# One multiplication of the feed-forward stage moved from GpSimd to VectorE, in a two-block transformer on one core

## The chip, the cores and the metric

The kernel runs on one core of a Trainium2 chip. The metric is the device time in microseconds, the median of the runs. A profiled execution also gives a trace of every engine: TensorE (PE, with its weight loads as PEld), VectorE (DVE), ScalarE (ACT), GpSimd (POOL) and the queue that issues transfers (SP).

## The reference, cut to what matters

Two transformer stacks of two layers each are computed one after the other in float32. The change lies in the feed-forward part of the first stack, which each of its two layers runs once:

```
hn = rms_norm(h, norm_ffn_g[l])
g, u = jnp.split(hn @ w_gu[l], [D_FF], axis=-1)
h = h + (jax.nn.silu(g) * u) @ w_down[l]
```

D_MODEL is 1024, D_FF is 2816 and there are 528 positions (16 meta tokens and 512 tokens; the second layer needs only the 512).

## The kernel before

Activations are stored transposed: 128 features on the partitions, positions along the row. A float32 product is made of three TensorE passes over operands split in a high and a low part (`mm3`, lines 96 to 98): high by high, high by low, low by high. Each split is a cast on ScalarE (`hi`) and a subtraction on VectorE (`lo`); for weights in `weight` that is L90 and L92, and in `split` L176 and L177.

D_FF is cut into 22 pieces of 128 features. `index(i)` makes piece i: gate and up product of it, silu of the gate, the product of the two, and its split into `yh` and `yl` for the down-projection. Pieces 0 to 2 are made in the plain way in `early`. Pieces 3 to 21 use the seven-product form: the gate and up weights and the two halves of the features and positions make a 2x2 by 2x2 block product, which needs seven block products instead of eight, at the price of sums of blocks.

- `halves4` loads the gate tile (r1) and the up tile (r2) of the piece and lets GpSimd make four sums of their blocks (L129 to L132). The sums go into `ws` and `ws4`, with one buffer each, and into r2 itself. Then r1, the sum `ws`, r2 and the sum `ws4` are split.
- `seven` runs the seven products, 12 matmuls of 264 (second layer: 256) columns each, in the order p1, p2, p6, p5, p7, p3, p4. p1 uses the PSUM bank "tr", p2, p5 and p3 use "mm" (three banks), and p6, p7 and p4 use "sc" (two banks). ScalarE copies p1 out (`u`, L159); VectorE adds the others up in the tile `quarters` (L161 to L172). p6 is taken out by L163, which also reads `u`. p4 gets the bank that p6 had.
- `index` then takes silu of the gate half on ScalarE (`sl`, L701, one buffer), multiplies it by the up half in place (L702), and splits the result into `yh` (ScalarE, L176) and `yl` (VectorE, L177).

The loop over `nf` in 5, 5, 4, 4, 4 makes one piece more than the down-projection needs next, and then runs the eight output tiles of the down-projection over `nf` pieces. So the seven-product forms come in runs of 3, 5, 4, 4 and 3 in each layer, with down-projections between them. Each engine works through its queue in order. The order in which the instructions of different pieces stand in a queue is fixed by a planner when the program is built; it need not be that of the source.

Of the kernel before, what the change touches and what calls it, by code (L numbers as in the profile page):

```python
# [46 lines left out]
def both_blocks(ctx: ExitStack, tc: tile.TileContext, xT, cst, par1, w1in, w1out, w1gu, w1dn, wgate,  # L47
                memT, pos, par2, rel, w2in, w2mix, w2mq, w2mkv, w2mo, w2f1, w2f2, out):
    nc = tc.nc
# [70 lines left out]
    def halves4(pool, w1, w2):  # L120


        r1 = wpool.tile([128, 8, 128], F32, name="wraw", bufs=3)
        nc.sync.dma_start(r1, w1)
        r2 = pool.tile([128, 8, 128], F32, name="wraw2", bufs=2)
        nc.sync.dma_start(r2, w2)
        s = pool.tile([128, 8, 128], F32, name="ws", bufs=1)
        s4 = pool.tile([128, 4, 128], F32, name="ws4", bufs=1)
        nc.gpsimd.tensor_add(s[:, 4:], r2[:, :4], r2[:, 4:])  # L129
        nc.gpsimd.tensor_sub(s[:, :4], s[:, 4:], r1[:, :4])  # L130
        nc.gpsimd.tensor_sub(r2[:, :4], r1[:, :4], r2[:, :4])
        nc.gpsimd.tensor_sub(s4, r1[:, 4:], s[:, :4])  # L132
        got = []
        for x in (r1, s, r2, s4):
            if x is s4:
                hi = pool.tile([128, 4, 128], F32R, name="wh4", bufs=1)
                lo = pool.tile([128, 4, 128], F32R, name="wl4", bufs=1)
            else:
                hi = wpool.tile([128, 8, 128], F32R, name="whi", bufs=3)
                lo = wpool.tile([128, 8, 128], F32R, name="wlo", bufs=3)  # L140
            split(hi, lo, x)
            got += [(hi[:, o:o + 4], lo[:, o:o + 4]) for o in range(0, hi.shape[1], 4)]
        return got

    def seven(pool, w, x, n, bufs):


        a11, a12, s2, s1, s3, a22, s4 = w
        b11, b21, t2, t1, t3, b22, t4 = x

        def product(ps, w, x):
            for k in range(4):
                mm3(ps, w[0][:, k], w[1][:, k], x[0][k], x[1][k], k == 0, k == 3)

        e = pool.tile([128, 4, n], F32, name="quarters", bufs=bufs)
        u = pool.tile([128, n], F32, name="u1", bufs=2)
        p1, p2, p6, p5, p7, p3, p4 = (bank(t)[:, :n] for t in ("tr", "mm", "sc", "mm", "sc", "mm", "sc"))
        product(p1, a11, b11)
        nc.scalar.copy(u, p1)  # L159
        product(p2, a12, b21)  # L160
        nc.vector.tensor_add(e[:, 0], p2, u)  # L161
        product(p6, s2, t2)
        nc.vector.tensor_add(e[:, 3], p6, u)  # L163
        product(p5, s1, t1)
        nc.vector.tensor_add(e[:, 1], p5, e[:, 3])
        product(p7, s3, t3)
        nc.vector.tensor_add(e[:, 2], p7, e[:, 3])
        nc.vector.tensor_add(e[:, 3], p5, e[:, 2])
        product(p3, s4, b22)
        nc.vector.tensor_add(e[:, 1], p3, e[:, 1])  # L170
        product(p4, a22, t4)
        nc.vector.tensor_add(e[:, 2], p4, e[:, 2])  # L172
        return e

    def split(hi, lo, x):
        nc.scalar.copy(hi, x)  # L176
        nc.vector.tensor_sub(lo, x, f(hi))  # L177
# [121 lines left out]
    for l in range(2):  # L299
# [3 lines left out]
        l0 = late[0][0]  # L303
        with ExitStack() as lay:
# [325 lines left out]
            with ExitStack() as ffn:  # L630
# [58 lines left out]
                def index(i):  # L689
                    if i < 3:  # L690
                        su = firsts[i][:, 2:4].rearrange("p a b -> p (a b)")
                    else:
                        with ExitStack() as order:
                            if i == 3:
                                for ins in after:
                                    order.enter_context(tc.issue_after(ins.ins))
                            w = halves4(ff, w1gu[l, 2 * i], w1gu[l, 2 * i + 1])
                        e = seven(ff, w, rhs, half, 3)
                        sg, su = (e[:, o:o + 2].rearrange("p a b -> p (a b)") for o in (0, 2))
                        sl = ff.tile([128, T], F32, name="sl", bufs=1)  # L700
                        nc.scalar.activation(sl[:, l0:], sg, AF.Silu)  # L701
                        nc.gpsimd.tensor_mul(su, su, sl[:, l0:])  # L702
                    hi = fy.tile([128, T], F32R, name=f"yh{i % 6}")
                    lo = fy.tile([128, T], F32R, name=f"yl{i % 6}")
                    split(hi[:, l0:], lo[:, l0:], su)
                    made.append((hi, lo))

                f0 = 0
                for nf in (5, 5, 4, 4, 4):
                    if l == 1 and f0 == 5:  # L710
                        tables()
                    while len(made) < min(f0 + nf + 1, 22):
                        index(len(made))
                    ys = made[f0:f0 + nf]
                    for m in range(8):
                        w = weight(w1dn[l, m, :, f0:f0 + nf], nf)
                        for p, a, b in proj(w, ys, late):
                            done = nc.vector.tensor_add(h[m][:, a:b], h[m][:, a:b], p)  # L718
                            if f0 + nf == 22 and m == 0:
                                ended = done  # L720
                    f0 += nf
# [619 lines left out]
```

## Time and profile before

| | |
|---|---|
| median of 3 runs | 2901.34 us (2901.32 to 2905.62) |
| the profiled execution, its own time | 2905.03 us |
| its span in the trace | 2903.2 us |
| PE busy | 2767.8 us (95%) |
| DVE busy | 1924.7 us (66%) |
| ACT busy | 1316.8 us (45%) |
| POOL busy | 679.7 us (23%) |

The median is what is forecast. The rows come from the profiled execution, so durations are compared with its own time. Busy shares are averages over stages with different limits. A busy PE is not PE at its peak, because matmuls overlap and their ends are modelled.

### The profile page before, as it was taken

The page shows a single profiled execution, that of the slowest core. Times are in us where ns is not written, and L with a number is a line of the kernel's source. Part 1 is how long each engine was busy: PE and PEld are TensorE (multiplying, and loading weights), DVE is VectorE, ACT ScalarE, POOL GpSimd, SP SyncE. Part 2 cuts the span into 40 slices and gives each one's busy share as a digit, 9 for nine tenths or more (in the row PEclk, how much of TensorE's full clock was granted, in tenths as well). Part 3 has the DMA queues.
Part 4 walks back from the last instruction along what each step waited for, and adds up shares of the span by engine and source line. Part 5 has one row for each costly group of instructions (what it writes and reads, how often), then busy time and mean ns, then how long its engine had stood idle before and what let it go on. Part 6 is the DMA issues. An engine that isn't in the chain of part 4 may idle for free.

```text
span 2903.2 us, 45359 instructions
## 1 busy us (share of the span) xinstructions
PE 2767.8 (95%) x17148; PEld 2445.7 (84%) x17148; DVE 1924.7 (66%) x3856; ACT 1316.8 (45%) x2362; POOL 679.7 (23%) x627
## 2 busy tenths in 40 slices
PE   8988999999998999999999999999999999999998
PEld 7988899999876888887789888888877898888887
DVE  7887756678888666667987564333689875643335
ACT  6664433336664433334675443332346754433323
POOL 0111544430012343432212031111322110311112
PEclk9999999999999999999999999999999999999999
DMA  4332223223332233335524223333245242233332
GB/s 149 83 82 88 67 89 94 88 80 103 97 88 84 82 93 89 90 92 141 157 64 129 87 66 95 97 98 96 80 131 148 64 133 81 66 102 94 95 94 66
DMA packets 101114, 277.35 MB, mean 96 GB/s; under 512 B 13856, under 2 KB 20512, under 8 KB 100896
## 3 DMA queue, kind: packets, MB, share of 16 engines
q1 hardware_dynamic: 100896, 274.45, 32.2%
q8 instruction: 136, 2.23, 0.3%
q14 instruction: 82, 0.67, 0.1%
HBM read 241.82 MB, written 2.10 MB: 84 GB/s over the span
## 4 chain that ended last, share of the span: by engine, by line
PE 57%; DVE 5%; issue 2%; ACT 2%; POOL 1%; ACTq 0%; POOLq 0%; DVEq 0%
PE mm L97 16%; PE mm L98 16%; PE mm L96 16%; PE sc L96 1%; PE sc L98 1%; PE sc L97 1%; DVE wlo L177 1%; PE av L96 1%; PE av L97 1%; PE av L98 1%; PE av L830 1%; PE bc L945 1%; PE tr L945 1%; DVE wlo L92 0%; ACT whi L176 0%
## 5 line engine op out<-in xcount | busy, mean ns | idle before, releaser
L96 PE MATMUL mm<-xh_all,whi 128*128 128x512 f32 (+2 forms) x2040 | 690.0, 341 | 18.9 <-ACT xh_all L316 8.1
L97 PE MATMUL mm<-xl_all,whi 128*128 128x512 f32 (+2 forms) x2040 | 694.3, 341 | 4.0 <-DVE xl_all L668 2.9
L98 PE MATMUL mm<-xh_all,wlo 128*128 128x512 f32 (+2 forms) x2040 | 688.4, 339 | 0.9 <-DVE wlo L92 0.8
L90 ACT CAST whi<-wraw 128x1024 fp32r<-128x1024 f32 (+2 forms) x416 | 391.3, 942 | 634.1 <-PE mm L97 587.7
L92 DVE TENSOR_TENSOR wlo<-wraw,whi 128x1024 fp32r<-128x1024 f32 (+2 forms) x393 | 460.4, 1172 | 212.9 <-ACT whi L90 210.4
L96 PEld LDWEIGHTS mm<-xh_all,whi 128*128 128x128 f32 x2040 | 390.5, 193 | 58.7 <-ACT xh_all L316 8.4
L97 PEld LDWEIGHTS mm<-xl_all,whi 128*128 128x128 f32 x2040 | 391.3, 192 | 43.6 <-DVE xl_all L668 5.1
L98 PEld LDWEIGHTS mm<-xh_all,wlo 128*128 128x128 f32 x2040 | 391.9, 192 | 36.0 <-DVE wlo L92 1.2
L1224 POOL TENSOR_TENSOR r<-r 128x512 f32<-128x512 f32 (+1 forms) x70 | 101.9, 1455 | 532.5 <-ACT r L1223 532.5
L96 PE MATMUL mm<-yh,whi 128*128 128x264 f32 (+1 forms) x528 | 169.7, 322 | 3.2 <-ACT yh L176 1.9
L97 PE MATMUL mm<-yl,whi 128*128 128x264 f32 (+1 forms) x528 | 169.9, 322 | 0.0
L98 PE MATMUL mm<-yh,wlo 128*128 128x264 f32 (+1 forms) x528 | 169.4, 321 | 0.0
L791 DVE TENSOR_TENSOR hall<-hall,mm 128x512 f32<-128x512 f32 (+1 forms) x82 | 46.6, 569 | 145.8 <-PE mm L98 145.5
L177 DVE TENSOR_TENSOR wlo<-wraw,whi 128x1024 fp32r<-128x1024 f32 x76 | 117.1, 1541 | 25.6 <-ACT whi L176 25.3
L96 PE MATMUL sc<-th,whi 128*128 128x264 f32 (+1 forms) x304 | 89.6, 295 | 31.7 <-DVE quarters L163 31.7
L96 PEld LDWEIGHTS mm<-yh,whi 128*128 128x128 f32 x528 | 99.0, 188 | 12.3 <-ACT yh L176 2.5
L97 PEld LDWEIGHTS mm<-yl,whi 128*128 128x128 f32 x528 | 99.2, 188 | 8.2 <-DVE yl L177 0.4
L98 PEld LDWEIGHTS mm<-yh,wlo 128*128 128x128 f32 x528 | 99.3, 188 | 8.0
L718 DVE TENSOR_TENSOR hall<-hall,mm 128x264 f32<-128x264 f32 (+1 forms) x120 | 61.1, 513 | 66.2 <-PE mm L98 65.9
L129 POOL TENSOR_TENSOR ws<-wraw 128x512 f32<-128x512 f32 x38 | 49.0, 1290 | 186.2 <-DVE wlo L177 117.0
L176 ACT CAST whi<-wraw 128x1024 fp32r<-128x1024 f32 x76 | 79.4, 1045 | 27.7 <-PE mm L97 26.0
L96 PEld LDWEIGHTS sc<-th,whi 128*128 128x128 f32 x304 | 58.7, 193 | 35.6 <-DVE quarters L163 35.4
(733 smaller groups left out, 7284.3 us busy)
## 6 DMA issues: line engine op xcount, KB each, us to landing
wraw<-w2f SPq DMA_DIRECT2D x128, 512.0 KB, 3.8
wraw<-w1gu SPq DMA_DIRECT2D x88, 512.0 KB, 3.6
wraw<-w2in SPq DMA_DIRECT2D x44, 512.0 KB, 4.0
wraw<-w1in SPq DMA_DIRECT2D x40, 512.0 KB, 3.6
wraw<-w2mkv SPq DMA_DIRECT2D x32, 512.0 KB, 3.6
wraw<-w1dn SPq DMA_DIRECT2D x48, 256.0 KB, 2.7
wraw<-w1dn SPq DMA_DIRECT2D x32, 320.0 KB, 3.0
wraw<-w1out SPq DMA_DIRECT2D x32, 256.0 KB, 2.7
```

The source lines that it names most:

```text
L90: nc.scalar.copy(hi[:, :kt], raw[:, :kt])
L92: (eng or nc.vector).tensor_sub(lo[:, :kt], raw[:, :kt], f(hi[:, :kt]))
L96: nc.tensor.matmul(ps, wh, xh, start=first, stop=False)
L97: nc.tensor.matmul(ps, wh, xl, start=False, stop=False)
L98: nc.tensor.matmul(ps, wl, xh, start=False, stop=last)
L129: nc.gpsimd.tensor_add(s[:, 4:], r2[:, :4], r2[:, 4:])
L176: nc.scalar.copy(hi, x)
L177: nc.vector.tensor_sub(lo, x, f(hi))
L718: done = nc.vector.tensor_add(h[m][:, a:b], h[m][:, a:b], p)
L791: nc.vector.tensor_add(X(m, a, b), X(m, a, b), p)
L945: nc.tensor.transpose(ps[:, 128 * j:128 * j + 128], p[:, 128 * j:128 * j + 128], ident)
L1224: nc.gpsimd.tensor_mul(r[:, a:b], r[:, a:b], r[:, a:b])
```

## The change

The multiplication of the silu of the gate by the up product (L702) is issued on VectorE instead of GpSimd, for the 19 pieces of each layer in the seven-product form. Operands, shapes and the place in the source stay.

```
                         sl = ff.tile([128, T], F32, name="sl", bufs=1)
                         nc.scalar.activation(sl[:, l0:], sg, AF.Silu)
-                        nc.gpsimd.tensor_mul(su, su, sl[:, l0:])
+                        nc.vector.tensor_mul(su, su, sl[:, l0:])
                     hi = fy.tile([128, T], F32R, name=f"yh{i % 6}")
                     lo = fy.tile([128, T], F32R, name=f"yl{i % 6}")
                     split(hi[:, l0:], lo[:, l0:], su)
```

## Rows read from the trace of the kernel before

**Rows 1.** The page: span, and busy time by engine.
```profile
span 2903.2 us, 45359 instructions
...
PE 2767.8 (95%) x17148; PEld 2445.7 (84%) x17148; DVE 1924.7 (66%) x3856; ACT 1316.8 (45%) x2362; POOL 679.7 (23%) x627
```
**Rows 2.** Windows: the runs of forms (a run, sums by layer), then products without waits.
```profile
core 0: us, PE busy (x) PEld busy (x) DVE busy (x) ACT busy (x) POOL busy (x), PEclk, DMA share, GB/s
...
391.64:449.26 57.62, 53.33 (x423) 52.69 (x421) 39.25 (x58) 23.52 (x33) 30.56 (x21) 0.97 0.28 81
...
sum 213.66, PE 199.93 PEld 197.79 DVE 150.81 ACT 88.56 POOL 106.25; mean PE 39.98 PEld 39.56 DVE 30.16 ACT 17.71 POOL 21.25
...
sum 216.48, PE 198.41 PEld 196.22 DVE 152.31 ACT 89.22 POOL 106.54; mean PE 39.68 PEld 39.24 DVE 30.46 ACT 17.84 POOL 21.31
...
401.89:409.19 7.30, 7.30 (x62) 7.30 (x61) 3.42 (x5) 2.38 (x4) 5.93 (x4) 1.00 0.26 74
1208.06:1213.78 5.72, 5.72 (x51) 5.72 (x49) 2.34 (x3) 1.45 (x2) 5.64 (x5) 1.00 0.30 82
```
**Rows 3.** Instructions of L163 (min/median/max ns), and who waited for them.
```profile
L163 DVE TENSOR_TENSOR quarters<-sc,u x38: 410/419/428, 337.0 to 1281.2; 128x264 f32<-128x264 f32 x19, 128x256 f32<-128x256 f32 x19
...
  PEld sc L96: 35.4, 18
  PE sc L96: 31.7, 18
```
**Rows 4.** TensorE at one stall: timeline, then windows after it (PEclk is third-last).
```profile
424.42 0.59 PE L96 MATMUL sc<-th,whi 128*128 128x264 f32 x1 [2.54 <-DVE quarters L163]
...
424.42:427.23 2.81, 2.81 (x13) 2.81 (x14) 2.73 (x6) 0.00 (x0) 1.06 (x1) 0.50 0.44 122
427.44:430.20 2.76, 2.76 (x24) 2.76 (x24) 2.20 (x3) 1.42 (x2) 2.68 (x3) 1.00 0.00 0
```
**Rows 5.** Timeline of GpSimd: start, duration, instruction, idle before it and releaser.
```profile
413.12 1.29 POOL L129 TENSOR_TENSOR ws<-wraw 128x512 f32<-128x512 f32 x1 [5.30 <-DVE wlo L177]
414.49 1.62 POOL L130 TENSOR_TENSOR ws<-ws,wraw 128x512 f32<-128x512 f32 x1
416.08 2.28 POOL L131 TENSOR_TENSOR wraw<-wraw,wraw 128x512 f32<-128x512 f32 x1
...
419.55 1.32 POOL L702 TENSOR_TENSOR quarters<-quarters,sl 128x528 f32<-128x528 f32 x1
426.17 1.28 POOL L129 TENSOR_TENSOR ws<-wraw 128x512 f32<-128x512 f32 x1 [5.29 <-DVE wlo L177]
```
**Rows 6.** Timeline of ScalarE in the same loop.
```profile
414.23 0.65 ACT L701 ACTIVATE sl<-quarters 128x528 f32<-128x528 f32 x1 [2.83 <-DVE quarters L170]
...
420.91 0.63 ACT L176 CAST yh<-quarters 128x528 fp32r<-128x528 f32 x1 [5.09 <-POOL quarters L702]
421.44 0.37 ACT L159 COPY u<-tr 128x264 f32<-128x264 f32 x1
```
**Rows 7.** Timeline of VectorE over two loops of the run from 391.64.
```profile
397.64 0.42 DVE L163 TENSOR_TENSOR quarters<-sc,u 128x264 f32<-128x264 f32 x1
...
398.70 1.22 DVE L177 TENSOR_TENSOR wlo<-ws,whi 128x1024 fp32r<-128x1024 f32 x1
...
402.09 0.43 DVE L172 TENSOR_TENSOR quarters<-sc,quarters 128x264 f32<-128x264 f32 x1 [0.18 <-PE sc L98]
403.09 2.30 DVE L177 TENSOR_TENSOR wlo<-wraw,whi 128x1024 fp32r<-128x1024 f32 x1 [0.57 <-ACT whi L176]
408.53 0.71 DVE L177 TENSOR_TENSOR yl<-quarters,yh 128x528 fp32r<-128x528 f32 x1 [3.13 <-ACT yh L176]
...
414.88 0.42 DVE L172 TENSOR_TENSOR quarters<-sc,quarters 128x264 f32<-128x264 f32 x1
...
423.94 0.43 DVE L163 TENSOR_TENSOR quarters<-sc,u 128x264 f32<-128x264 f32 x1
```
**Rows 8.** Groups by line: first matmuls of the down-projection, with their idle time.
```profile
L96 PE MATMUL mm<-yh,whi 128*128 128x264 f32 (+1 forms) x528 | 169.7, 322 | 3.2 <-ACT yh L176 1.9 <-DVE hall L718 1.3
```

More of the change, by code (lines that the diff above doesn't have):

```diff
@@ L701, in index @@
                         nc.scalar.activation(sl[:, l0:], sg, AF.Silu)
-                        nc.gpsimd.tensor_mul(su, su, sl[:, l0:])
+                        nc.vector.tensor_mul(su, su, sl[:, l0:])
                     hi = fy.tile([128, T], F32R, name=f"yh{i % 6}")
```

## The prediction

> **What bounds the kernel now.** I read the page first: TensorE is busy for 95% of the span, VectorE for 66% [rows 1]. The share says little about the stage of the change, so I turned to the two gate-and-up stages and timed the runs of seven-product forms on TensorE. A layer has 19 forms in five runs (3, 5, 4, 4 and 3 forms; between runs TensorE does the down-projection). The ten runs take 213.66 + 216.48 = 430.1 us [rows 2]. Where nothing is waited for, five products of layer 0 take 7.30 us, 1.46 each, and four of layer 1 take 5.72 us, 1.43 each [rows 2]. At that pace a form takes 7 x 1.46 = 10.2 us, and 38 forms take 133 x 1.46 + 133 x 1.43 = 384.4 us. So the runs hold 430.1 - 384.4 = 45.8 us that is not product work. This is the sum that the change can win, and it is 1.6% of the span.
>
> Who takes it: TensorE waits 18 times, 31.7 us in all (35.4 us by its weight loads), for L163 on VectorE [rows 3]. L163 empties the "sc" bank of the third product, and the seventh product needs that bank. In the large case TensorE idles 2.54 us, and then its granted clock is 0.50 (the 1.2 GHz level) for the next 2.81 us before it is 1.00 again [rows 4]; the twelve products' matmuls that need 1.46 us took those 2.81, so such a stall costs 1.35 us more. Of the 45.8 us, 35.4 are the waits; the other 10.4 are mostly such slow stretches (one is shown), and I allow 2 us of them for losses that have nothing to do with this loop.
>
> Why L163 is late: follow one loop backwards. L163 at 423.94 [rows 7] needs the copy u of the first product (L159). On ScalarE u stands in the queue right behind the cast yh, and yh waits 5.09 us for L702 [rows 6]. L702 starts at 419.55, directly behind the four sums of weights that stand ahead of it on GpSimd since 413.12 (6.43 us) [rows 5]. Its inputs were long there: sl (L701) was done at 414.88 [rows 6] and L172 at 415.30 [rows 7]. L702 itself takes 1.32 us. The next sums start at 426.17, because `ws` has one buffer, and wait for the VectorE split of the sums before [rows 5]. So the loop is sums, L702, yh, u, L161 to L163, split of ws, sums: 426.17 - 413.12 = 13.05 us, against the 10.2 us of TensorE. The loop sets the pace, and 18 loops with all four sums make the 18 stalls.
>
> **The change, part by part.** *GpSimd* loses 38 x 1.32 = 50 us of L702. GpSimd is not a bound by share; what counts is that its sums no longer stand ahead of the product.
>
> *VectorE* gains 38 multiplications of 128x528 (128x512 in layer 1), SBUF by SBUF. The nearest row is yl, the same shape and operands: 0.71 us, some 0.65 before the next one starts [rows 7]. That is 38 x 0.65 = 25 us on an engine that is idle for a third of the span. In a loop VectorE has now from 408.53 to 415.30 (6.8 us, 0.4 of it idle or held), plus one split wlo of 1.2: 7.6 us. With the product it has 8.2 us, under 10.2, so by its own work it stays hidden. If it were not, 0.65 would be added per loop.
>
> *The place on VectorE.* The queue's order before shows L172, the split wlo of the next form's third weight (403.09), yl [rows 7]. The product can only stand after L172 and before yl. Either place costs the same below. Its input sl is done when L172 ends, so it waits for nothing new, and yh follows it 4 to 5 us earlier than now, u directly behind.
>
> *Where the stall goes: the two engines' hold on each other.* A VectorE instruction with two SBUF operands and a GpSimd instruction do not run together here. L131 takes 2.28 us instead of L129's 1.29 when a wlo is in its way [rows 5], and wlo takes 2.30 instead of 1.22 when a sum is in its way [rows 7]. No longer hold is in these rows: each is held by one instruction of the other engine, then goes. L163, which reads PSUM, is never held: 410 to 428 ns over 38 [rows 3]. So the moved product meets the sums. The Trainium skill ("SBUF — State Buffer", section "SBUF: two separate sides") calls this an exclusive lock on a shared port pair, in which the loser blocks for the whole instruction, and this is a rule against the change; the trace agrees with it (2.30 against 1.22 us), and a rival below works out its worst case.
>
> I walk the run from 391.64 with turns taken one by one. The split of ws ends at 399.92 [rows 7] and L129 runs 400.06 to 401.36. L172 is 402.09 to 402.52. L130 ends at 403.03; the product is held until then and runs to 403.65. L131 runs to 404.90, wlo to 406.05, L132 to 407.30, yl to 407.90 (yh was done long before). Then come L161, wlo of the next first weight, and L163, ending at about 409.95. From the end of the split of ws to its next end is 11.5 us: 8.2 of own work and some 3.3 of holds. The seventh product wants L163 at 391.64 + 8.76 + 10.2 = 410.6, so the first loop has 0.65 us to spare (the 2.3 us lead that L163 of the first form had, ending 398.06 against 400.4 [rows 2, 7], absorbs the lag). The second loop then is 11.5 - 10.2 = 1.3 late, less 0.65: 0.6 us; a third is 1.3 late. A run of 3 has one full loop, of 4 two, of 5 three. So a layer keeps 0 + 1.9 + 0.6 + 0.6 + 0 = 3.1 us, two layers 6.2; with the 2 us that are not of this loop, 8 us stay. None of these stalls is as long as the 2.54 us that the slow clock followed, so the clock's part goes whole.
>
> *Ends of runs.* The down-projection waits 1.9 us in all for a yh [rows 8]; the product on VectorE ends about 0.65 us sooner and is not held by or behind sums. I take 1 us.
>
> *Bounds.* No row shows how the two engines share when the queues are this full. From below: if GpSimd always gives way, no loop is over 10.2 and the whole 45.8 plus 1.9 is won, 48 us. From above: no loop has lead, 18 x 1.3 = 23 us stay, and 22 us are won. The walk lies nearest to the first, as it uses this run's own rows: 45.8 - 8 + 1 = 39 us.
>
> **Does it reach the end?** TensorE is busy through 95% of the span [rows 1], and nothing outside the two stages is edited, so I let what TensorE gains there stay gained. The order of each queue is written when the program is built, from a plan that the trace does not show; I allow a few us either way for orders that change elsewhere.
>
> **The sum.** The profiled execution took 2905.0 us (span 2903.2 [rows 1] and 1.8 around it). 2905.0 - 39 = 2866. That execution is 3.7 us above the median of 2901.34, so on the median the forecast is **2862 us**.
>
> **Rivals.**
> (a) *The loop opens only in part.* yh may be queued on ScalarE behind a cast that waits for a sum (the casts of ws and wh stand near it). Then u still waits for some of the sums, about half of the 6.43 us, and half the gain is left: 2901 - 20 = 2881. For it: the order on ScalarE is not known. Against: yh becomes ready 4 us before those casts.
> (b) *No change: the holds take the place of the wait.* If all four sums hold VectorE for their whole length, the loop is 8.2 + 4 x 1.29 = 13.4 us, about today's 13.05, and the time is 2901 within 6. By the page's lock rule taken at its worst, this is the outcome. Against: L129 runs beside L167 to L170, which read PSUM and are not held, and part of L130 beside L172.
> (c) *Slower: VectorE paces every form, not only 18.* Today 20 forms lose almost nothing. If held-up VectorE work made all 38 run at one loop, the break-even is 10.2 + 45.8 / 38 = 11.4 us a form. At 11.5 it is 38 x 1.3 = 49 us of loss instead of 45.8, 3 us slower; at 13.4 it is 122 us, 2977 in all. For it: the walk's 11.5 is just over the point. Against: TensorE waits in only 18 of the 38 forms today [rows 3]; for the others the sums were made during the down-projection, or the next run's are not wanted yet, so nothing holds VectorE.
>
> **How the numbers follow.** Gain of 30 to 48 us: 0.70. Part of it, 6 to 30 us (a): 0.16. Within 0.2% (6 us, about what a measurement of this kernel can tell from no change) (b): 0.08. Slower (c), or by a worse order elsewhere: 0.06. So faster 0.86, same 0.08, slower 0.06. The range runs from the full 48 us (2853, less a us for scatter) to just past (a), at 2882; it leaves out some 2 in 10, nearly all above.
>
> **What would show it.** Right: L702 on VectorE at about 0.7 us, up to 2 when held; the ten runs together some 392 us instead of 430; waits of TensorE for L163 under 10 us and none above 2 us; granted clock 1.00 all through the runs; L129's starts in a run 10.2 to 11.5 us apart. Wrong: starts still 13 us apart (b), or yh on ScalarE still waiting 4 to 5 us (a), or waits in the first and last forms of the runs (c), or the runs shorter as said and the span not.

## The result, and the profile after

The changed kernel takes 2863.38 us (median of 4 runs, 2862.56 to 2867.84) against 2901.72 us before (4 runs, 2901.32 to 2905.62). The ratio is 0.9868, with a 95% interval of 0.9851 to 0.9885: 38.3 us less, where 39 were forecast. The profiled execution took 2867.84 us.

The first lines of the page of the changed kernel. VectorE gained 47 us of busy time [rows 1], more than the 25 us of its new instructions; the rest is holding, as below.

```profile
span 2866.1 us, 45365 instructions
...
PE 2761.2 (96%) x17148; PEld 2441.0 (85%) x17148; DVE 1971.8 (69%) x3894; ACT 1322.1 (46%) x2362; POOL 638.5 (22%) x589
```

Windows of its runs of seven-product forms: the run of five in layer 0, the first run of layer 1, and the sum for each layer (the third number from the right is the granted clock).

```profile
390.05:441.91 51.86, 51.43 (x423) 51.21 (x421) 47.20 (x62) 24.13 (x33) 26.82 (x17) 1.00 0.31 93
...
sum 196.12, PE 195.20 PEld 194.56 DVE 174.63 ACT 90.65 POOL 92.41; mean PE 39.04 PEld 38.91 DVE 34.93 ACT 18.13 POOL 18.48
...
952.45:984.07 31.62, 30.92 (x255) 30.20 (x253) 29.37 (x44) 16.60 (x25) 10.26 (x7) 1.00 0.32 93
...
sum 193.75, PE 191.88 PEld 190.19 DVE 177.91 ACT 91.47 POOL 92.87; mean PE 38.38 PEld 38.04 DVE 35.58 ACT 18.29 POOL 18.57
```

The ten runs take 196.12 + 193.75 = 389.9 us, where they took 430.1 [rows 2]. That is 40.3 us less, and 389.9 - 384.4 = 5.5 us that are not product work are left of 45.8. The granted clock is 1.00 in all ten. TensorE's waits for L163, by the view of that line, fell from 31.7 to 2.5 us [rows 3]:

```profile
  PEld sc L96: 4.1, 7
...
  PE sc L96: 2.5, 5
```

The same loop in the timelines of GpSimd, ScalarE and VectorE (start, duration, instruction, idle before and releaser):

```profile
409.60 1.29 POOL L129 TENSOR_TENSOR ws<-wraw 128x512 f32<-128x512 f32 x1 [4.19 <-DVE wlo L177]
410.97 1.64 POOL L130 TENSOR_TENSOR ws<-ws,wraw 128x512 f32<-128x512 f32 x1
412.57 1.76 POOL L131 TENSOR_TENSOR wraw<-wraw,wraw 128x512 f32<-128x512 f32 x1
414.28 2.27 POOL L132 TENSOR_TENSOR ws<-wraw,ws 128x512 f32<-128x512 f32 x1
420.74 1.29 POOL L129 TENSOR_TENSOR ws<-wraw 128x512 f32<-128x512 f32 x1 [4.19 <-DVE wlo L177]
...
413.21 0.64 ACT L176 CAST yh<-quarters 128x528 fp32r<-128x528 f32 x1 [0.91 <-DVE quarters L702]
413.75 0.37 ACT L159 COPY u<-tr 128x264 f32<-128x264 f32 x1
...
411.37 0.42 DVE L172 TENSOR_TENSOR quarters<-sc,quarters 128x264 f32<-128x264 f32 x1
411.89 1.28 DVE L702 TENSOR_TENSOR quarters<-quarters,sl 128x528 f32<-128x528 f32 x1
413.10 2.31 DVE L177 TENSOR_TENSOR wlo<-wraw,whi 128x1024 fp32r<-128x1024 f32 x1
415.33 1.79 DVE L177 TENSOR_TENSOR yl<-quarters,yh 128x528 fp32r<-128x528 f32 x1
...
418.51 0.42 DVE L163 TENSOR_TENSOR quarters<-sc,u 128x264 f32<-128x264 f32 x1
```

The product follows L172 at once, yh waits 0.91 us instead of 5.09 [rows 6], and L129's starts are 11.14 us apart instead of 13.05 [rows 5]. Now three VectorE instructions in a row meet the sums and are each held by one of them: 1.28 instead of 0.71 us, 2.31 instead of 1.22, 1.79 instead of 0.71.

### The profile page after: what moved, and what is told of

Read it like the earlier page. It is cut to its first block, busy times and chain, and to the rows that moved or that the text cites. A ratio compares the mean times of both kernels' runs of the same rounds, so it can differ in the third digit from the quotient of the medians.

```text
span 2866.1 us, 45365 instructions
## 1 busy us (share of the span) xinstructions
PE 2761.2 (96%) x17148; PEld 2441.0 (85%) x17148; DVE 1971.8 (69%) x3894; ACT 1322.1 (46%) x2362; POOL 638.5 (22%) x589
## 4 chain that ended last, share of the span: by engine, by line
PE 59%; DVE 5%; issue 1%; ACT 1%; POOL 0%; ACTq 0%; POOLq 0%; DVEq 0%
PE mm L97 17%; PE mm L98 16%; PE mm L96 16%; PE sc L96 1%; PE sc L98 1%; PE sc L97 1%; PE av L96 1%; PE av L97 1%; PE av L98 1%; PE av L830 1%; PE tr L945 1%; PE bc L945 1%; DVE wlo L92 0%; PE sc L951 0%; PE sc L952 0%
## 5 line engine op out<-in xcount | busy, mean ns | idle before, releaser
L92 DVE TENSOR_TENSOR wlo<-wraw,whi 128x1024 fp32r<-128x1024 f32 (+2 forms) x393 | 452.1, 1151 | 209.8 <-ACT whi L90 207.0
L130 POOL TENSOR_TENSOR ws<-ws,wraw 128x512 f32<-128x512 f32 x38 | 57.7, 1519 | 202.3 <-DMA wraw<-w1gu 200.1
L129 POOL TENSOR_TENSOR ws<-wraw 128x512 f32<-128x512 f32 x38 | 49.1, 1291 | 168.4 <-DVE wlo L177 98.4
```

The source lines that it names most:

```text
L92: (eng or nc.vector).tensor_sub(lo[:, :kt], raw[:, :kt], f(hi[:, :kt]))
```

## The experiments

Times are medians, beside the kernel before on the same chip (2903.1 us for the first four, 2901.7 for the next four, 2902.4 for the last three).

**The product first on GpSimd.** It stays there at full length, but the sums of the form after next are queued behind it:

```
-                made = []
+                made, muls = [], {}
...
-                            if i == 3:
-                                for ins in after:
+                            if i == 3 or i - 2 in muls:
+                                for ins in after if i == 3 else [muls[i - 2]]:
                                     order.enter_context(tc.issue_after(ins.ins))
...
+                        muls[i] = nc.gpsimd.tensor_mul(su, su, sl[:, l0:])
```

> The product stays on GpSimd, at its full 1.3 us, but stands ahead of the next sums in GpSimd's queue instead of behind them. Nothing else changes its place. Theory (the place in the queue behind four sums is the cost): the casts yh stop waiting 5 us, L129 starts 10.2 to 11.5 us apart instead of 13.05, TensorE's waits for L163 fall from 31.7 us to under 10, and the time is 2858 to 2875 us, about what the move to VectorE gave (2863). Rival 1 (what counts is that the product takes 0.7 us on VectorE instead of 1.3): little is won, 2890 us or more. Rival 2 (what counts is that GpSimd no longer holds VectorE with the product): little is won too, 2890 us or more, since GpSimd still runs it.

Measured: 2869.53 us, ratio 0.9888 (0.9871 to 0.9904). The order of the four other queues is that of the kernel before. GpSimd in this kernel, then the sums over the windows of the runs, layer 0 and layer 1:

```profile
399.14 1.32 POOL L702 TENSOR_TENSOR quarters<-quarters,sl 128x528 f32<-128x528 f32 x1 [6.03 <-DVE quarters L172]
400.43 2.27 POOL L129 TENSOR_TENSOR ws<-wraw 128x512 f32<-128x512 f32 x1
...
410.75 1.32 POOL L702 TENSOR_TENSOR quarters<-quarters,sl 128x528 f32<-128x528 f32 x1 [1.87 <-DVE quarters L172]
...
sum 197.63, PE 196.38 PEld 194.91 DVE 171.49 ACT 86.59 POOL 127.93; mean PE 39.28 PEld 38.98 DVE 34.30 ACT 17.32 POOL 25.59
...
sum 195.45, PE 192.53 PEld 190.36 DVE 172.65 ACT 87.55 POOL 128.03; mean PE 38.51 PEld 38.07 DVE 34.53 ACT 17.51 POOL 25.61
```

The product now stands ahead and waits for its own input, L172. The loop is 410.75 - 399.14 = 11.6 us and the runs take 197.63 + 195.45 = 393.1 us. So the place in the queue, without a change of engine or duration, wins 37 of the runs' 40 us. Both rivals are out.

**Half the product.** On GpSimd, behind the sums, with half of its columns left out:

```
+                        nc.gpsimd.tensor_mul(su[:, :half], su[:, :half], sl[:, l0:l0 + half])
```

> The product stays on GpSimd behind the sums, but multiplies only the first half of the columns; the other half is left out. Its time falls from 1.3 to some 0.7 us, as on VectorE. Theory (place in the queue): the loop gets 0.6 us shorter, 13.05 to 12.4, so of the 18 stalls 0.6 us each goes, 11 us, with a few us more where a shorter stall no longer brings the slow clock: 2880 to 2893 us. Rival 1 (the shorter duration is the gain): 2860 to 2870 us.

Measured: 2893.4 us, ratio 0.9965 (0.9953 to 0.9976), 0.4 us above the range of the theory. L702 takes 0.76 us here, and it is as late as before:

```profile
409.64 1.29 POOL L129 TENSOR_TENSOR ws<-wraw 128x512 f32<-128x512 f32 x1 [5.30 <-DVE wlo L177]
...
416.06 0.76 POOL L702 TENSOR_TENSOR quarters<-quarters,sl 128x264 f32<-128x264 f32 x1
422.11 1.29 POOL L129 TENSOR_TENSOR ws<-wraw 128x512 f32<-128x512 f32 x1 [5.29 <-DVE wlo L177]
```

The loop is 12.47 us. The shorter duration alone is worth about a quarter of the gain. The few us that the theory added for the clock did not come: five of the ten runs here still have a granted clock below 1.00, against six in the kernel before.

**The split behind u and L163.** The product stays on GpSimd, as late as before; its split is traced after L163 of the next form and queued behind u and L163:

```
         nc.vector.tensor_add(e[:, 3], p6, u)
+        if then:
+            with tc.issue_after(copied.ins), tc.issue_after(added.ins):
+                then()
```

> The product stays on GpSimd behind the sums, but the split of its result (yh on ScalarE, yl on VectorE) stands behind the copy u and behind L163 of the next form in those queues. The product is as late as before. Theory (the late product costs only because u, L161 and L163 are queued behind its split): L163 no longer waits for the product, the loop loses u, L161, the split of the first weight and L163, some 2.6 us, and comes to about 10.4 us, and the time is 2858 to 2875 us. Rival (the late product costs by something else, such as the buffers or the down-projection that wants yh): no gain, 2895 us or more.

Measured: 2902.1 us, ratio 0.9995 (0.9986 to 1.0004). The expectation failed. The timelines of ScalarE and VectorE show why (the casts and splits of `split` are L179 and L180 here):

```profile
421.06 0.63 ACT L179 CAST yh<-quarters 128x528 fp32r<-128x528 f32 x1 [4.81 <-POOL quarters L705]
421.60 1.04 ACT L179 CAST whi<-wraw 128x1024 fp32r<-128x1024 f32 x1
...
417.29 0.42 DVE L161 TENSOR_TENSOR quarters<-mm,u 128x264 f32<-128x264 f32 x1
422.68 1.23 DVE L180 TENSOR_TENSOR wlo<-wraw,whi 128x1024 fp32r<-128x1024 f32 x1 [4.96 <-ACT whi L179]
423.82 0.43 DVE L163 TENSOR_TENSOR quarters<-sc,u 128x264 f32<-128x264 f32 x1
```

u and L161 are early now. But behind yh stands the cast of the next first weight as well, and VectorE's split of that weight stands ahead of L163. So there are two ways from the late yh to L163, and I had named one. The rows before hold a third: yl, which waits for yh, stood ahead of L161 and L163 on VectorE [rows 7]. This edit moved yl behind L163 as well, so what that way costs by itself is not shown.

**The split behind the next weights too.** As before, but handed to `halves4` two forms later:

```
-            split(hi, lo, x)
+            ops = split(hi, lo, x)
+            if x is s and then:
+                with tc.issue_after(ops[0].ins), tc.issue_after(ops[1].ins):
+                    then()
```

> The product stays on GpSimd behind the sums. Its split (yh, yl) stands behind not only u and L163 of the next form, but also behind the casts and splits of the first weight and of the sum of the form after it. The trace of the run that moved the split behind u and L163 alone shows that yh still stood ahead of the cast of the next first weight on ScalarE, and that VectorE's split of that weight, for which L163 stands in line, waited 5 us for it. Theory, widened (all that stands behind yh on ScalarE is late with it, the casts of weights as well as u): with those ahead of yh too, the loop opens, and the time is 2858 to 2878 us. Rival (the product's lateness costs by something that is not in ScalarE's queue, so that only an earlier product helps): no gain, 2895 us or more.

Measured: 2859.06 us, ratio 0.9853 (0.9838 to 0.9868), with the product (L704 here) on GpSimd and still behind its sums. GpSimd in the run of five, then the sums over the windows of the runs, layer 0 and layer 1:

```profile
412.76 2.27 POOL L132 TENSOR_TENSOR ws<-wraw,ws 128x512 f32<-128x512 f32 x1
414.98 2.32 POOL L704 TENSOR_TENSOR quarters<-quarters,sl 128x528 f32<-128x528 f32 x1
418.52 1.29 POOL L129 TENSOR_TENSOR ws<-wraw 128x512 f32<-128x512 f32 x1 [1.22 <-DVE wlo L179]
...
sum 194.80, PE 194.69 PEld 194.48 DVE 163.80 ACT 90.77 POOL 118.11; mean PE 38.94 PEld 38.90 DVE 32.76 ACT 18.15 POOL 23.62
...
sum 190.31, PE 190.25 PEld 189.86 DVE 165.66 ACT 91.15 POOL 118.45; mean PE 38.05 PEld 37.97 DVE 33.13 ACT 18.23 POOL 23.69
```

These are 385.1 us, 0.7 over the runs' own work. Here a late product costs nothing that the runs show, once nothing that TensorE needs soon is queued behind its split.

**One layer alone.** The product on VectorE in layer 0 only:

```
+                        (nc.gpsimd if l else nc.vector).tensor_mul(su, su, sl[:, l0:])
```

> The product is on VectorE in the first layer only. Theory: the effects are local to each layer's runs, so the runs of layer 0 take 196 us instead of 214, those of layer 1 stay at 216, and the time is 2901.7 - 17.6 = 2884 us (2881 to 2887). Rival (the plan elsewhere or the clock gives part of the gain): runs as said, but a time that is off by over 4 us.

Measured: 2885.33 us, ratio 0.9938 (0.9923 to 0.9953). Layer 0's runs take 196.14 us. Layer 1's take 213.33, 3 us less than before and than expected. Its second and third run here, and after them the same two in the kernel before:

```profile
1014.93:1072.00 57.07, 50.72 (x422) 50.10 (x420) 38.58 (x58) 23.28 (x33) 30.57 (x21) 1.00 0.28 80
1100.02:1144.07 44.05, 40.47 (x337) 40.06 (x336) 31.59 (x46) 18.22 (x26) 22.89 (x16) 1.00 0.26 76
...
1030.70:1089.17 58.47, 52.11 (x422) 51.49 (x420) 38.77 (x58) 23.30 (x33) 30.58 (x21) 0.97 0.28 82
1117.19:1162.70 45.51, 41.93 (x337) 41.52 (x336) 31.70 (x46) 18.20 (x26) 22.84 (x16) 0.96 0.26 77
```

Before, these two took 58.47 and 45.51 us, at a granted clock of 0.97 and 0.96. TensorE idles as long here (6.35 and 3.58 us, against 6.36 and 3.58), but no slow stretch followed its stalls. So that part of the gain is not tied to a stall each time. The rest of the effect is local to each layer.

**The product twice.** A second multiplication on VectorE in each form, whose result nobody uses:

```
                         nc.vector.tensor_mul(su, su, sl[:, l0:])
+                        nc.vector.tensor_mul(sl[:, l0:], su, sl[:, l0:])
```

> The changed kernel with a second multiplication of the same size on VectorE in each of the 38 forms (its result is not used). Theory (VectorE is near its limit only in the loops with all four sums, by its own work and the holds): each of the 18 loops gets 0.65 to 1.2 us longer, 11.1 to some 12, and the time is 2870 to 2885 us, so by 8 to 21 us more than the changed kernel. Rival c (VectorE paces every form): 38 x 0.65 to 1.2, 25 to 45 us more, 2888 us or over. Rival (VectorE has room and the sums are what paces the loop): under 4 us more.

Beside it, and for the next experiment, the changed kernel ran again:

> The changed kernel again, beside the others on one chip. Both theories: 2861 to 2866 us.

Measured: 2870.82 us beside 2863.56 for the changed kernel, ratios 0.9888 (0.9873 to 0.9903) and 0.9865 (0.9849 to 0.9882). The difference of 7.3 us is just under what the theory said, and far from the 25 us or more of rival (c). L163 in the run of five, then the sums over the windows of the runs, layer 0 and layer 1:

```profile
407.57 0.42 DVE L163 TENSOR_TENSOR quarters<-sc,u 128x264 f32<-128x264 f32 x1
...
419.32 0.42 DVE L163 TENSOR_TENSOR quarters<-sc,u 128x264 f32<-128x264 f32 x1
...
sum 200.64, PE 196.08 PEld 194.80 DVE 182.59 ACT 90.51 POOL 92.38; mean PE 39.22 PEld 38.96 DVE 36.52 ACT 18.10 POOL 18.48
...
sum 198.47, PE 192.23 PEld 190.36 DVE 184.70 ACT 91.29 POOL 92.91; mean PE 38.45 PEld 38.07 DVE 36.94 ACT 18.26 POOL 18.58
```

The loop is 11.75 us against 11.13 (407.38 to 418.51) in the changed kernel. So VectorE does pace the loops with all four sums, by 0.62 us for 0.65 of work, but only those: the ten runs take 200.64 + 198.47 = 399.1 us, 9.2 more than in the changed kernel, which is 0.5 for each of the 18 loops, where 0.62 in all 38 forms would be 23.6. The runs are the better measure here than the time, because the order of TensorE's matmuls differs in the stages behind them.

**The silu in PSUM, in layer 1.** The product there has one operand in PSUM:

```
+                        if l == 1:
+                            sl = bank("av")
+                            nc.scalar.activation(sl, sg, AF.Silu)
+                            nc.vector.tensor_mul(su, su, sl)
```

> The changed kernel, but in layer 1 the silu of the gate is written to a PSUM bank, so that the product there has one operand in PSUM and one in SBUF; layer 0 is as it was. Theory (VectorE is held by GpSimd only where both operands are in SBUF): in layer 1 the product takes 0.7 us each time instead of up to 1.28, the loops there get 0.5 us shorter, the runs of layer 1 take 191 us instead of 193.75, and those of layer 0 stay at 196; the time falls by 2 to 3 us, at the edge of what can be measured. Rival (the hold goes by the time at which the two engines meet, whatever the operands): products in layer 1 still up to 1.28 us, runs unchanged.

Measured: 2860.24 us, ratio 0.9856 (0.9842 to 0.9871). That is 3.3 us under the changed kernel, which is inside the scatter; the trace decides. The product in layer 1 (min/median/max ns), one of them and the sum on GpSimd at that moment, then the sums over the runs of both layers:

```profile
L703 DVE TENSOR_TENSOR quarters<-quarters,av x19: 686/689/690, 965.0 to 1244.1; 128x512 f32<-128x512 f32 x19
...
1021.41 0.69 DVE L703 TENSOR_TENSOR quarters<-quarters,av 128x512 f32<-128x512 f32 x1
...
1020.37 1.63 POOL L130 TENSOR_TENSOR ws<-ws,wraw 128x512 f32<-128x512 f32 x1
...
sum 196.12, PE 195.22 PEld 194.58 DVE 174.56 ACT 90.64 POOL 92.39; mean PE 39.04 PEld 38.92 DVE 34.91 ACT 18.13 POOL 18.48
...
sum 190.42, PE 190.35 PEld 189.85 DVE 170.45 ACT 91.96 POOL 92.17; mean PE 38.07 PEld 37.97 DVE 34.09 ACT 18.39 POOL 18.43
```

All 19 products take 0.69 us, though nine of them run while a sum runs on GpSimd; in the changed kernel they take up to 1.28. Layer 0 is unchanged, and layer 1 goes from 193.75 to 190.42 us, where its products alone need 190.2. So the hold goes by the operands, and the hold on the product is behind nearly all the waiting that is left in layer 1. The Trainium skill ("SBUF — State Buffer", section "SBUF: two separate sides") has the lock only for VectorE instructions in a two-port mode or with two SBUF inputs, and the trace agrees (0.69 us against up to 1.28).

**A version that beats both?** The kernel with the product on GpSimd and its split last had the shortest runs. I ran it again, with the changed kernel beside it, and with both edits at once (its product on VectorE).

> Both at once: the product on VectorE, and its split behind the casts and splits of the next weights. Theory: the run with the product on GpSimd and the split last already has its ten runs of products at 385 us, against 384.4 without any wait, so nothing is left to win there, and the product on VectorE only adds holds: 2858 to 2863 us. Rival (the two gains add up): 2850 us or less.

> The product on GpSimd with its split last, again, in more rounds and beside the changed kernel on the same chip. Theory: 2857 to 2862 us, 2 to 5 us under the changed kernel, since its runs of products are 4.5 us shorter. Rival (the lower time of the first run was the chip's scatter): within 1 us of the changed kernel.

> The changed kernel, for comparison on the same chip: 2861 to 2866 us.

Measured: both at once 2861.47 us (0.9855, 0.9841 to 0.987); the split last 2861.51 us (0.9863, 0.9847 to 0.9879); the changed kernel 2860.46 us (0.9859, 0.9844 to 0.9873). The gains do not add up, as the theory said. The split last has 385.1 us of runs again and the changed kernel 389.5, but the 4 us between them do not show in the time, against what was expected: so the first run's 2859 against 2863.6 can be scatter as well. No version is shown to beat the changed kernel.

## Why the prediction was right, point by point

**What bounds the kernel: right.** The loop through the product's place behind the sums set the pace. The first experiment opens it by the place alone, and half a product opens it by 0.6 us only. One reading was wrong: the 35.4 us are the waits of the weight loads. TensorE itself idled 213.66 - 199.93 + 216.48 - 198.41 = 31.8 us in the runs [rows 2], so 14.0 of the 45.8 us, and not 10.4, were matmuls at less than their full pace. After the change, 2.8 us of idling and 2.7 of slower matmuls are left. The sum to be won stays as it was.

**The way to L163: right in its end, too narrow in its middle.** The prediction led from yh to u to L163. There is a second way, from yh to the cast of the next first weight, to its split, to L163, which the failed run showed and the run after it closed, and a third through yl on VectorE. The number did not depend on this, since an early product opens them all.

**The walk: right in kind.** It gave 11.5 us a loop, 8.2 of own work and 3.3 of holds. Measured: 11.14, of which the three held instructions, and 0.2 on the split of ws4, make 0.57 + 1.09 + 1.08 + 0.2 = 2.9 of holds, and 8.2 own work is left. The turns came one by one, as assumed. The mis-sized term is the rest that stays: 8 us were taken, 5.5 measured, and its parts are further off than their sum. With the 0.4 us shorter loop the first run of four in layer 0 takes 40.93 us for 28 x 1.46 = 40.88 of products, so it keeps 0.05 us where 0.6 were given, and the run of five keeps 51.86 - 51.1 = 0.8 where 1.9 were given. But the first runs of three, which were given nothing, keep 31.71 - 30.66 = 1.05 us in layer 0 and 31.62 - 30.03 = 1.6 in layer 1. In layer 1 the product with an operand in PSUM takes 0.9 us of that away (that run is 30.69 us there); where the rest comes from is not shown.

**Ends of runs: right in kind.** TensorE's wait for yh at the down-projection, 1.9 us before [rows 8], no longer shows in its row, where 1 us of gain was taken; its weight loads still wait 0.6. Whether this reached the time cannot be told from the few us by which executions differ.

```profile
L96 PE MATMUL mm<-yh,whi 128*128 128x264 f32 (+1 forms) x528 | 169.7, 322 | 1.6 <-DVE hall L718 1.5
L96 PEld LDWEIGHTS mm<-yh,whi 128*128 128x128 f32 x528 | 99.0, 188 | 10.5 <-DVE hall L718 1.9 <-ACT yh L176 0.6
```

**The clock: right in its outcome, not in its reason.** The granted clock is 1.00 in all ten runs. The reason given was that no stall left is as long as the 2.54 us that the slow clock followed. The half product shows a stall of 2.00 us that it followed as well (last section), so that length is no bound. The longest stall left in the runs for L163 is 0.65 us.

**Reaching the end: right within scatter.** The runs lost 40.3 us and the profiled span 37.1. Outside the runs the span is 2903.2 - 430.1 = 2473.1 us before and 2866.1 - 389.9 = 2476.2 after. A second profile of the changed kernel has 2861.1 - 389.65 = 2471.5 there, at a mean granted clock of 0.987 instead of 0.984. So these few us differ between executions of one kernel. That the forecast median of 2862 lies 1.4 us from the measured one is therefore in part luck: the runs won 40.3 us where the prediction gave them 37.8, and medians of the changed kernel lie between 2860.5 and 2863.6.

**The plan elsewhere: within what was allowed.** ScalarE's and SP's queues are in the same order before and after. On VectorE the new instruction stands where it was put, and two additions of the down-projection change places with a yl. Around the end of the first layer's feed-forward part (655.8 to 682.8 us before) 69 places of VectorE's queue hold another instruction than before, and TensorE's order differs in 19 of 17148 matmuls. No cost of this shows: the first experiment, with the old order in all queues but GpSimd's, spends 2864.7 - 393.1 = 2471.6 us outside the runs, and the changed kernel 2471.5 to 2476.2.

**The rivals.** (a) did not come: yh waits 0.9 us. (b) came in part: holds cost 2.9 us of the 13.05 - 8.2 = 4.85 that they would have needed. (c) is true only in the loops with all four sums; there VectorE sets the pace, as the doubled product shows.

## What to carry to other kernels

An instruction on a lightly used engine can set the pace of the busiest one, if it stands behind work that is not urgent and something urgent is queued behind its reader. Follow the queue on each engine in both directions: the remedy may be another engine, an earlier place, or a later place for the reader, and here each of the three gave the same 1.1 to 1.5%. When only one of several ways was cleared, nothing was won here (ratio 0.9995), so look at what else stands behind the late instruction before trusting a chain.

## What the runs showed of the hardware that was not expected

A stall of the same length is not always followed by the slow clock. In the kernel before, the stall of 2.54 us that ended at 424.42 was followed by a granted clock of 0.50, the 1.2 GHz level [rows 4]. Another of 2.54 us, which ended at 582.08, was followed by full clock, while after the one that ended at 511.66 the clock fell about 1 us late (0.79 over the first 1.94 us, then 0.50):

```profile
511.66:513.60 1.94, 1.94 (x13) 1.94 (x14) 1.89 (x3) 0.00 (x0) 0.19 (x1) 0.79 0.45 135
513.60:516.20 2.60, 2.60 (x13) 2.60 (x13) 2.02 (x6) 1.58 (x2) 1.56 (x2) 0.50 0.00 0
...
582.10:584.00 1.90, 1.90 (x15) 1.90 (x16) 1.86 (x3) 0.00 (x0) 0.17 (x1) 1.00 0.47 136
584.00:588.00 4.00, 4.00 (x35) 4.00 (x34) 3.42 (x6) 2.06 (x3) 2.45 (x2) 1.00 0.00 1
```

A shorter stall can be followed by it too. In the kernel with half the product TensorE idled 2.00 us until 432.84, and 1 us later its clock fell:

```profile
432.84 0.40 PE L96 MATMUL sc<-th,whi 128*128 128x264 f32 x1 [2.00 <-DVE quarters L163]
...
433.86:437.20 3.34, 3.34 (x17) 3.34 (x17) 2.85 (x6) 1.51 (x2) 1.58 (x2) 0.50 0.22 84
```

What decides between them was not tried.
